# Splits of early projection rows, tap transposes and one rotary half moved in an attention and convolution layer pair

## The chip, the cores and the metric

The kernel runs on one core of a Trainium2 chip. The metric is the time of one execution on the device in microseconds (us). Before the change three runs took 1692.68 to 1693.34 us, with a median of 1692.94 us. Besides, one execution was taken by the hardware profiler; every row of a view below is from that one.

## The reference

Two layers work on 1024 latent tokens of width 1024, with a prefix of 256 context tokens. Layer 0 is an attention layer: 16 query heads of 128, four key and value heads (a group of four query heads shares one), a window of 128 tokens to each side, all context keys in the same softmax, a learned sink logit for each head, and rotary positions on latent queries and keys. Layer 1 is a convolution module of width 2048 with 31 taps. Each layer is normalised and modulated before its input projection, and a SiLU gate path multiplies its result before the output projection.

```python
def attention_layer(h_lat, h_ctx, w_in, sink, w_out, cos, sin, ctx_out):
    ...
    proj = h_lat @ w_in
    q = apply_rope(split_heads(proj[..., :q_end], N_Q_HEADS), cos, sin)
    k = apply_rope(split_heads(proj[..., q_end:k_end], N_KV_HEADS), cos, sin)
    ...
    o = windowed_attention(q, k, v, kc, vc, sink)
    y = (o * jax.nn.silu(z)) @ w_out
    return y, y_ctx
```

All inputs are float32. The kernel computes a product of two float32 matrices as three TensorE products: each operand is split into a high part, which is a rounded copy, and a low part, which is what the copy left out; then high times high, high times low and low times high are added up in one PSUM bank.

## The kernel before

**Engines and order.** TensorE (PE in the profile) multiplies and transposes, ScalarE (ACT) makes the rounded high copies and the exponentials, VectorE (DVE) the low parts, maxima and evacuations, GpSimd (POOL) the low parts of weights, the normalising of the softmax and most of the rotary arithmetic, SyncE (SP) issues nearly all DMAs. The order of PE's instructions is the order in which the program writes them (`pin`, L106). The orders on the other engines, after the start, are set by the planner of the framework, which runs a model of the engines' times at build time. The program can tie two instructions of one engine: `after` (L624) makes an instruction come behind a named one in that engine's queue. Each engine works its queue in order, so an instruction that waits holds all that stand behind it.

**Buffers.** Tiles of 128 x 1024 floats come from 45 pages, `pg` (L115), tiles of half that size from six half pages, `hp` (L116). Both hand out the page that has been free longest. PSUM has two banks `psg` for projections, two double banks `pss` for scores and transposed softmax rows, and two banks `pso`.

**The start.** Modulated inputs are made for the two halves of the latent tokens. For the second half a row of scales is spread over all partitions in the half page `rb` (L580); `x_f` (L455) reads it, and it is freed at L1184. The first head's query, key and value are projected here, and their rotary halves use the half pages too.

**The attention steps.** The loop at L1226 runs over 16 heads and eight blocks of 128 queries. A step writes on PE: the scores of the next block (`scores`, L1032), 12 matmuls of waiting work (`fill`, L1019), a value stage where one is due (`pv`, L1102), and the transposes of this block's softmax rows (`transposes`, L1068). After the transposes ACT copies the high part out of PSUM into `pthi`, and DVE writes the low part into `ptlo`; `anchor_a` and `anchor` name the last such pair of copies, `anchor_z` the two instructions that evacuate the latest half of a gate (L948). The waiting work is the projection of the next heads' queries and gates; `job` (L986) does 24 matmuls for each half of the tokens and calls `finish` (L934). For queries and keys that is `rope` (L896): ACT copies the bank, two DMAs swap the halves of a head, DVE multiplies by the cosine, POOL by the sine, then comes an addition and a low part. For queries after the first head both of the last two are on POOL. Where a new group of four heads begins (heads 4, 8 and 12) its key and value are projected in one go, 72 matmuls each.

**The output projection of layer 0** (`proj_attn`, L718) runs over four sub-sweeps `s` (half of the tokens by half of the columns) and eight row pairs `kk` of the weight; `i` counts both. `split(i)` (L735) makes the high part of a weight pair (`woh`) and, in the sub-sweeps where new rows of the attention's result come in, the high and low part of those rows (`ozh`, `ozl`), which were stored to DRAM and loaded again as `ozf`. `block` multiplies. The first seven row pairs (`EARLY_ROWS`) of the first sub-sweep begin early, as waiting work in the last head's steps: of their four blocks two are multiplied there (`early_proj`, L874), in the two banks `psg`, the other two afterwards. In that first pass `split(i + 1)` is written with the products of pair `i`.

**The taps.** The 31 taps of the convolution are loaded as rows and must be transposed. `turn_taps(q)` (L1298), four times, transposes four tiles of 32 rows into a bank `pso`, and DVE copies it into `dww`; the fourth time two sums follow. The four calls wait in the list `later`. `bgA` (L1800) is called after each row pair and takes up to two of them, from row pair 2 of a sub-sweep on. With two `pso` banks the third call needs a bank that the first has used.

Of the kernel before, what the change touches and what calls it, by code (L numbers as in the profile page):

```python
# [94 lines left out]
def backbone_kernel(  # L95
# [452 lines left out]
    for kt in range(2, KT):  # L548
        nx = kt + 1
        if 2 < kt < KT - 1:  # L550
            ada_row(nx)
            tp = turn(xs0, nx, ps_g)
        if kt == 5:
            root1 = rstd_root(ss1, D, 4)
        if kt == KT - 1:
            x_mm(kt - 1, 0, acc0, (2,))
            turn_vecs()
        x_mm(kt, 0, acc0, (0,))
        if nx < KT:
            ada_cols(nx)  # L560
            if kt == 5:
                r1 = rstd_end(root1, 4)
            x_tile(tp, nx, 0, V)
        else:
            x_h(0)
            x_f(1)
            x_l(0)
            rc = rstd_end(rootc, 2)
        x_mm(kt, 0, acc0, (1,) if nx < KT else (2, 1))
        if nx < KT:  # L570
            x_mm(kt - 1, 0, acc0, (2,), range(3) if kt > 2 else (1, 2))
        for i in {3: (0, 1), 4: (2, 3)}.get(kt, ()):
            square(xs1[i], ss1[:, i:i + 1], A)
        if kt == 4:
            pg.free(*xs1)
        if kt == 5:
            rps = ps_o(1)
            for b in range(4):
                PE.matmul(rps[:, b * P:b * P + P], r1[:, b:b + 1].to_broadcast([P, P]), ident, start=True, stop=True)
            rb_pg = hp.alloc(F32, None, "rb")  # L580
            rb1 = rb_pg[:, 0:512]
            act(rb1, rps, AF.Copy)
            for i in range(2):
                square(cx[i], ssc[:, i:i + 1], A)
        if kt == 6:
            pg.free(*xs0)
            cos, sin = (pg.alloc(F32, [1024], n) for n in ("cos", "sin"))
            SY.dma_start(out=cos, in_=k_cos)
            SY.dma_start(out=sin, in_=k_sin)
            rootc = rstd_root(ssc, D, 2)  # L590
            x_f(0)
# [126 lines left out]
    def proj_attn():  # L718

        st, oz = {}, {}  # L720
        todo = {"load": 0, "split": 0}

        def load(i):
            s, kk = seqB[i]
            h, m = subs[s]
            w, wl = pg.alloc(F32, [2, 512], "wo"), pg.alloc(F32R, [2, 512], "wol")
            SY.dma_start(out=w, in_=pair_rows(Wo, m, kk))
            SY.dma_start(out=wl.bitcast(F32), in_=wolA[m, kk])
            st[i] = [w, wl]
            if m == 0:  # L730
                f = pg.alloc(F32, [2, 512], "ozf")
                SY.dma_start(out=f, in_=ozd[2 * kk:2 * kk + 2, :, h * 512:h * 512 + 512].rearrange("a p n -> p a n"))
                oz[(h, kk)] = f

        def split(i):  # L735
            s, kk = seqB[i]
            h, m = subs[s]
            w, wl = st[i]
            wh = pg.alloc(F32R, [2, 512], "woh")
            act(wh, w, AF.Copy)  # L740
            pg.free(w)
            st[i] = (wh, wl)
            if m == 0:
                f = oz[(h, kk)]
                oh, ol = pg.alloc(F32R, [2, 512], "ozh"), pg.alloc(F32R, [2, 512], "ozl")
                after(act(oh, f, AF.Copy), anchor_z[0:1] if i else [])
                after(split_lo(V, ol, f, oh), anchor_z[1:2] if i else [])
                pg.free(f)
                oz[(h, kk)] = (oh, ol)

        def ahead(i, nl, ns):
            while todo["load"] <= min(i + nl, len(seqB) - 1):
                load(todo["load"])
                todo["load"] += 1
            while todo["split"] <= min(i + ns, len(seqB) - 1):
                split(todo["split"])
                todo["split"] += 1

        def block(s, kk, b, acc, w, o):
            for e in range(2):  # L760
                lh, ll = (t[:, e, b * P:b * P + P] for t in o)
                for a, c in ((lh, w[0]), (lh, w[1]), (ll, w[0])):
                    PE.matmul(acc, a, c[:, e], start=kk == 0 and e == 0 and a is lh and c is w[0],
                              stop=kk == NK - 1 and e == 1 and a is ll)
                    yield

        for i in range(EA):
            ahead(i, 0, -1)
            yield
        ahead(0, 1, 0)  # L770
        yield
        banks = {4: ps_g(), 5: ps_g()}
        for i in range(EARLY_ROWS):
            ahead(i, min(EA, EARLY_ROWS - 1 - i), min(1, EARLY_ROWS - 1 - i))
            for b in range(2):
                yield from block(0, i, b, banks[4 + b], st[i], oz[(0, i)])
        yield "early"
        ta, tb = ps_s(), ps_s()
        for i in range(4):
            banks[i] = (ta, tb)[i // 2][:, i % 2 * 512:i % 2 * 512 + 512]  # L780
        held = []
        xr = None
        for i, (s, kk) in enumerate(seqB):
            h, m = subs[s]
            acc = [banks[b] for b in ((4, 5, 0, 1), (2, 3, 4, 5), (0, 1, 4, 5), (2, 0, 3, 1))[s]]
            ahead(i, EA, 0)
            if kk == 4:
                xr = [pg.alloc(F32, [2, 512], "xr") for _ in range(2)]
                for b in range(4):
                    SY.dma_start(out=xr[b // 2][:, b % 2],  # L790
                                 in_=x[0, (4 * h + b) * P:(4 * h + b + 1) * P, m * 512:m * 512 + 512])
            w, o = st.pop(i), oz[(h, kk)]
            if i >= len(seqB) - BYBLOCK:
                ahead(i, EA, 1)
                held.append((kk, w, o))
                bgA(s, kk)
                if kk == NK - 1:
                    for b in range(4):
                        for k2, w, o in held:
                            run(block(s, k2, b, acc[b], w, o))  # L800
                        evac0(s, b, acc[b], xr)
                    for k2, w, o in held:
                        pg.free(*w, *o)
                continue
            for b in range(2 if i < EARLY_ROWS else 0, 4):
                run(block(s, kk, b, acc[b], w, o))
                if b == 2:
                    ahead(i, EA, 1)
            pg.free(*w)
            if m:  # L810
                pg.free(*oz.pop((h, kk)))
            bgA(s, kk)
            if kk == NK - 1:
                for b in range(4):
                    evac0(s, b, acc[b], xr)
# [77 lines left out]
            PE.matmul(o, wl[:, kt], Hh[kt][:, sl], start=False, stop=kt == KT - 1)  # L893
            yield

    def rope(o, sl, d, ropes=None, hold=None):  # L896
        qe, qs = (hp.alloc(F32, None, "rope") for _ in range(2))
        m = (hp if ropes is None else pg).alloc(F32, None, "rope")
        e, w, r = qe[:, 0:512], qs[:, 0:512], m[:, 0:512]
        act(e, o, AF.Copy)  # L900
        queue = A if ropes is None else SY
        queue.dma_start(out=w[0:64], in_=e[64:128])
        queue.dma_start(out=w[64:128], in_=e[0:64])
        first = tt(V, r, o, cos[:, sl], ALU.mult)
        tt(G, w, w, sin[:, sl], ALU.mult)

        def add(behind=None):
            i = tt(G if ropes is None and hold is None else V, r, r, w, ALU.add)
            if behind:
                after(i, [behind])  # L910
            act(d[0][:, sl], r, AF.Copy)

        def low():
            split_lo(G if ropes is None else V, d[1][:, sl], r, d[0][:, sl])
            hp.free(qe, qs)
            (hp if ropes is None else pg).free(m)

        def rest(behind):
            add(behind)
            low()  # L920

        if hold is not None:
            while hold:
                hold.pop()(first)
            hold.append(rest)
        elif ropes is None:
            add()
            low()
        else:
            ropes.extend((add, low))  # L930
# [3 lines left out]
    def finish(kind, n, half, o, d, ropes=None, hold=None):  # L934
# [8 lines left out]
                    hold.pop()(i)  # L943
                return None
        if kind in "qk":
            return rope(o, sl, d, ropes, hold)
        if kind == "z":
            anchor_z[:] = [act(d[:, sl], o, AF.Tanh, scale=0.5), stt(d[:, sl], d[:, sl], 1.0, o, ALU.add, ALU.mult)]  # L948
            return None
# [226 lines left out]
    for kt in range(KT):  # L1176
# [4 lines left out]
        if kt + 3 < KT:  # L1181
            x_f(kt + 3)
        if kt + 3 == KT - 1:
            hp.free(rb_pg)  # L1184
        if kt < 2:
            finished0(0, acc0, (kt,), ropes0)
        if kt > 3 and ropes0:
# [612 lines left out]
    def bgA(s, kk):  # L1800
        if s == 2 and kk == 6:
            wsB.load()
            wsB.load()
        if s == 3 and kk >= 5:
            wsB.split()
        for _ in range(2 if kk >= 2 else 0):
            if later:
                later.popleft()()

# [96 lines left out]
```

## Time and profile before

| | |
|---|---|
| median of three runs | 1692.94 us |
| the profiled execution, its own time | 1694.15 us |
| its span, from the first to the last instruction | 1692.4 us |
| TensorE busy | 1676.4 us (99%) |
| VectorE, ScalarE, GpSimd busy | 1115.4, 880.9 and 881.3 us |
| granted TensorE clock, mean | 0.998 |

A row of the timeline has the start in us from the beginning of the span, the duration in us, the engine, the line, the operation, the tiles (result, then operands), the shape, and how many like instructions the row stands for. In brackets stands how long the engine was idle before, and what released it. All instructions show L89, because a helper records them; they are told apart by their tiles. The list of waits gives the total in us, the number and the longest. The times of matmuls are pipelined and their ends are modelled, so one matmul overlaps the next.

### The profile page before, as it was taken

How to read it: one execution, taken by the hardware profiler on the slowest of the kernel's cores; microseconds unless marked ns; L12 is line 12 of the kernel's file. 1: busy time of each engine (PE TensorE's matmuls, PEld its weight loads, DVE VectorE, ACT ScalarE, POOL GpSimd, SP SyncE). 2: the span in 40 equal slices, each digit the busy share in tenths (PEclk: the TensorE clock that was granted, in tenths of full speed). 3: DMA queues.
4: the chain of work that ended last, by engine and by line, in shares of the span. 5: the costliest groups of instructions: out<-in, count | busy, mean ns of one | idle time of the engine just before them, and what ended most of it. 6: DMA issues, size and time to landing. Idle time of an engine off the chain costs nothing.

```text
span 1692.4 us, 23973 instructions
## 1 busy us (share of the span) xinstructions
PE 1676.4 (99%) x8436; PEld 1414.4 (84%) x8436; DVE 1115.4 (66%) x2120; ACT 880.9 (52%) x1556; POOL 881.3 (52%) x730
## 2 busy tenths in 40 slices
PE   9999999999999999999999999999999999999998
PEld 6788888888888888888788888888888888888886
DVE  4755554556356644566224289999999999868832
ACT  5755553555355543556234365555665654566741
POOL 0256663666466673652001268999898888130400
PEclk9999999999999999999999999999999999999999
DMA  9424442544344443447876623010211202377881
GB/s 387 148 80 143 143 126 84 163 144 141 92 139 151 147 133 99 134 136 247 288 253 220 229 82 101 13 64 25 75 50 51 82 32 82 126 272 245 315 292 50
DMA packets 114775, 244.54 MB, mean 144 GB/s; under 512 B 11626, under 2 KB 36514, under 8 KB 114656
## 3 DMA queue, kind: packets, MB, share of 16 engines
q1 hardware_dynamic: 108576, 233.06, 40.7%
q10 hardware_dynamic: 6080, 9.97, 2.4%
q8 instruction: 66, 1.08, 0.3%
q14 instruction: 53, 0.43, 0.1%
HBM read 190.80 MB, written 41.69 MB: 137 GB/s over the span
## 4 chain that ended last, share of the span: by engine, by line
PE 92%; DMA 4%; DVE 2%; ACT 1%; issue 0%; SPq 0%; POOL 0%; ACTq 0%; DVEq 0%; POOLq 0%
PE psg L89 49%; PE pss L89 23%; PE pso L89 21%; DMA x_page<-in_x_dram 1%; DMA x_page<-in_ctx_dram 1%; DMA araw_page<-in_k_ada_dram 1%; DMA wo_page<-in_attn_w_out_dram 0%; DMA rope_half<-rope_half 0%; DMA ozf_page<-ozd 0%; DVE hf_page L89 0%; DMA dww_raw<-in_ada_w_dram 0%; DVE ozl_page L89 0%; DVE oz_half L89 0%; ACT x_page L89 0%; ACT hh_page L89 0%
## 5 line engine op out<-in xcount | busy, mean ns | idle before, releaser
L89 POOL TENSOR_TENSOR odd_half<-odd_half,prod_half 128x513 f32<-128x513 f32 (+2 forms) x252 | 315.0, 1257 | 22.0 <-ACT prod_half L89 8.6
L89 PE MATMUL psg<-hh_page,whi_page 128*128 128x512 f32 x600 | 235.7, 393 | 0.0
L89 PE MATMUL psg<-hl_page,whi_page 128*128 128x512 f32 x600 | 234.7, 391 | 0.0
L89 PE MATMUL psg<-hh_page,wlo_page 128*128 128x512 f32 x600 | 234.2, 390 | 0.0
L89 POOL TENSOR_TENSOR wlo_page<-wraw_page,whi_page 128x512 fp32r<-128x512 f32 (+1 forms) x104 | 171.9, 1668 | 115.7 <-ACT whi_page L89 50.3
L89 ACT ACTIVATE prod_half<-ubuf,dww 128x513 f32<-128x513 f32 (+2 forms) x252 | 165.7, 675 | 115.8 <-POOL odd_half L89 111.9
L89 PE MATMUL psg<-h2h_page,whi_page 128*128 128x512 f32 x464 | 182.1, 392 | 0.0
L89 PE MATMUL psg<-h2h_page,wlo_page 128*128 128x512 f32 x464 | 180.9, 390 | 0.0
L89 PE MATMUL psg<-h2l_page,whi_page 128*128 128x512 f32 x464 | 180.8, 390 | 0.0
L89 POOL TENSOR_SCALAR p_page<-p_page,sc 128x640 f32<-128x640 f32 (+1 forms) x128 | 100.5, 786 | 148.6 <-DVE sc L89 134.2
L89 DVE SCALAR_TENSOR_TENSOR pss<-ubuf,dww,pss 128x512 f32<-128x512 f32 (+3 forms) x270 | 172.5, 671 | 0.1
L89 DVE SCALAR_TENSOR_TENSOR pss<-ubuf,wsum,pss 128x512 f32<-128x512 f32 (+3 forms) x270 | 171.8, 671 | 0.2
L89 ACT ACTIVATE p_page<-p_page,sc 128x641 f32<-128x641 f32 (+1 forms) x128 | 102.9, 804 | 93.2 <-DVE sc L89 90.3
L89 ACT ACTIVATE pthi<-pss 128x512 fp32r<-128x512 f32 (+2 forms) x144 | 87.4, 618 | 111.6 <-PE pss L89 108.0
L89 DVE TENSOR_TENSOR ptlo<-pss,pthi 128x512 fp32r<-128x512 f32 (+2 forms) x144 | 101.9, 716 | 63.0 <-ACT pthi L89 61.7
L89 PEld LDWEIGHTS psg<-hh_page,wlo_page 128*128 128x128 f32 x600 | 112.8, 188 | 24.4
L89 PEld LDWEIGHTS psg<-hh_page,whi_page 128*128 128x128 f32 x600 | 112.9, 188 | 19.2
L89 PEld LDWEIGHTS psg<-hl_page,whi_page 128*128 128x128 f32 x600 | 112.9, 188 | 18.4
L89 POOL TENSOR_TENSOR rope_half<-rope_half,sin_page 128x512 f32<-128x512 f32 x40 | 52.0, 1300 | 132.3 <-DMA rope_half<-rope_half 60.3
L89 ACT ACTIVATE whi_page<-wraw_page 128x1024 fp32r<-128x1024 f32 x88 | 92.6, 1052 | 51.1 <-PE psg L89 21.4
L89 PE MATMUL pso<-h2h_page,wlo_page 128*128 128x512 f32 x304 | 118.4, 389 | 0.0
L89 PE MATMUL pso<-h2h_page,whi_page 128*128 128x512 f32 x304 | 118.4, 389 | 0.0
(257 smaller groups left out, 4074.1 us busy)
## 6 DMA issues: line engine op xcount, KB each, us to landing
wraw_page<-in_k_wconv_dram SPq DMA_DIRECT2D x48, 512.0 KB, 3.3
wraw_page<-in_k_win_dram SPq DMA_DIRECT2D x40, 512.0 KB, 3.7
wo_page<-in_attn_w_out_dram SPq DMA_DIRECT2D x32, 512.0 KB, 5.7
wol_page<-wolA SPq DMA_DIRECT2D x32, 512.0 KB, 8.6
wo_page<-in_conv_w_out_dram SPq DMA_DIRECT2D x32, 512.0 KB, 7.2
wol_page<-wolC SPq DMA_DIRECT2D x32, 512.0 KB, 6.4
rope_half<-rope_half ACTq DMA_DIRECT2D x76, 128.0 KB, 2.3
araw_page<-in_k_ada_dram SPq DMA_DIRECT2D x16, 512.0 KB, 10.1
```

The source lines that it names most:

```text
L89: r = f(*a, **k)
```

## The change

- The row `rb` takes a full page instead of a half page.
- `split(i)` no longer ties the parts of the attention rows to the last gate half in every call but the first. For row pairs 1 to 6, and only these, the high part on ACT is tied behind the evacuation of the latest gate half and behind the latest `pthi` copy, the low part on DVE behind the second instruction of that evacuation and the latest `ptlo`.
- `rope` gets an engine for its addition and its low part. It is VectorE for the second half of the tokens of queries 4, 8 and 12, and GpSimd as before for the other queries.
- `bgA` takes from `later` in the first sub-sweep from row pair 0 on, so that the four tap transposes go with row pairs 0 and 1 instead of 2 and 3.

```diff
@@ -577,7 +577,7 @@
-            rb_pg = hp.alloc(F32, None, "rb")
+            rb_pg = pg.alloc(F32, [1024], "rb")
...
@@ -743,8 +743,11 @@
                 oh, ol = pg.alloc(F32R, [2, 512], "ozh"), pg.alloc(F32R, [2, 512], "ozl")
-                after(act(oh, f, AF.Copy), anchor_z[0:1] if i else [])
-                after(split_lo(V, ol, f, oh), anchor_z[1:2] if i else [])
+                high, low = act(oh, f, AF.Copy), split_lo(V, ol, f, oh)
+                if 0 < i < EARLY_ROWS:
+                    for ins, ties in ((high, (anchor_z[0:1], anchor_a)), (low, (anchor_z[1:2], anchor))):
+                        for t in ties:
+                            after(ins, t)
...
@@ -893,7 +896,7 @@
-    def rope(o, sl, d, ropes=None, hold=None):
+    def rope(o, sl, d, ropes=None, hold=None, eng=G):
...
@@ -905,13 +908,13 @@
-            i = tt(G if ropes is None and hold is None else V, r, r, w, ALU.add)
+            i = tt(eng if ropes is None and hold is None else V, r, r, w, ALU.add)
...
-            split_lo(G if ropes is None else V, d[1][:, sl], r, d[0][:, sl])
+            split_lo(eng if ropes is None else V, d[1][:, sl], r, d[0][:, sl])
...
@@ -943,7 +946,7 @@
-            return rope(o, sl, d, ropes, hold)
+            return rope(o, sl, d, ropes, hold, V if kind == "q" and half and n and n % 4 == 0 else G)
...
@@ -1181,7 +1184,7 @@
-            hp.free(rb_pg)
+            pg.free(rb_pg)
...
@@ -1803,7 +1806,7 @@
-        for _ in range(2 if kk >= 2 else 0):
+        for _ in range(2 if kk >= 2 or s == 0 else 0):
             if later:
                 later.popleft()()
```

## The prediction

> **What bounds the kernel now.** I read the page first, then the busy times by stretch, then who TensorE (PE) waited for, then the timeline around each wait.
>
> ```profile
> span 1692.4 us, 23973 instructions
> PE 1676.4 (99%) x8436; PEld 1414.4 (84%) x8436; DVE 1115.4 (66%) x2120; ACT 880.9 (52%) x1556; POOL 881.3 (52%) x730
> ```
>
> ```profile
> 0.00:45.00 45.00, 41.89 (x297) 29.40 (x297) 22.55 (x56) 26.99 (x42) 1.12 (x7) 1.00 0.97 388
> 772.00:831.00 59.00, 56.11 (x299) 46.79 (x298) 27.13 (x54) 26.96 (x41) 8.39 (x18) 1.00 0.81 269
> 831.00:1448.00 617.00, 617.00 (x2754) 511.15 (x2752) 505.01 (x822) 326.42 (x471) 422.65 (x310) 1.00 0.30 103
> 1530.00:1693.00 163.00, 154.37 (x706) 128.66 (x704) 89.87 (x173) 79.38 (x135) 23.48 (x16) 0.98 0.65 229
> ```
>
> The columns are the stretch, its length, and the busy time of PE, its weight loads, VectorE (DVE), ScalarE (ACT) and GpSimd (POOL), then the granted clock. PE is busy for 1676.4 of 1692.4 us, so only its 16 us of idle time, and what overlaps a modelled end, can be won. Of those, 8.63 us lie in the last stretch (163.00 - 154.37) and 3.11 in the first 45 us, where the change does almost nothing. From 831 to 1448 PE has no idle time at all. The one other stretch that loses is 772 to 831: 59.00 - 56.11 = 2.89 us. There the first row pairs of the output projection are mixed into the last attention steps. The pace of products of 512 columns, from the chain that ended last, is 43.52 / 192 = 0.227 us:
>
> ```profile
> 934.93 43.52 PE pss L89 x192
> ```
>
> ```profile
> PE pso L89 <- DVE dww L89: 1.4, 1, 1.4
> PE pss L89 <- DVE ptlo L89: 1.1, 1, 1.1
> PE pso L89 <- ACT hf_page L89: 0.8, 2, 0.6
> PE psg L89 <- DVE zs_page L89: 0.4, 1, 0.4
> ```
>
> Three of these waits, dww, ptlo and zs, are in that stretch. A wait is less exact than the distance between starts, so I price them by starts.
>
> **Row pairs 1 to 6: the splits behind the softmax copies.** PE, then ScalarE (ACT), then DVE:
>
> ```profile
> 230.84 0.59 PE L89 MATMUL pso<-mask_page,ones 128*1 128x256 f32 x2
> 231.36 0.39 PE L89 MATMUL pss<-kh_page,qh_page 128*128 128x256 f32 x1
> ...
> 780.85 0.71 PE L89 MATMUL pss<-ident,p_page 128*128 128x128 f32 x5
> ...
> 786.32 0.59 PE L89 MATMUL pso<-mask_page,ones 128*1 128x256 f32 x2
> 788.00 0.44 PE L89 MATMUL pss<-kh_page,qh_page 128*128 128x384 f32 x1 [1.09 <-DVE ptlo L89]
> ...
> 791.71 0.40 PE L89 MATMUL pso<-pthi,kvc_page 128*128 128x512 f32 x1
> 792.18 0.51 PE L89 MATMUL pso<-ptlo,kvc_page 128*128 128x512 f32 x1
> ```
>
> ```profile
> 783.31 1.99 ACT L89 ACTIVATE ozh_page<-ozf_page 128x1024 fp32r<-128x1024 f32 x2
> 785.21 0.68 ACT L89 ACTIVATE pthi<-pss 128x640 fp32r<-128x640 f32 x1
> ```
>
> ```profile
> 784.85 2.36 DVE L89 TENSOR_TENSOR ozl_page<-ozf_page,ozh_page 128x1024 fp32r<-128x1024 f32 x2
> 787.12 0.82 DVE L89 TENSOR_TENSOR ptlo<-pss,pthi 128x640 fp32r<-128x640 f32 x1
> ...
> 791.32 0.81 DVE L89 TENSOR_TENSOR ptlo<-pss,pthi 128x640 fp32r<-128x640 f32 x1
> ```
>
> PE's scores at 788.00 wait for `ptlo`, the low softmax copy of a step that PE had transposed by 781.6. It is late because ACT ran two row-pair splits (`ozh`, 1.99 us) ahead of the high copy `pthi`, and DVE two more (`ozl`, 2.36 us) ahead of `ptlo`. The new ties keep each split of pairs 1 to 6 behind both copies of the step emitted last. So `pthi` can run where ACT started `ozh`, from 783.3 to 784.0, and `ptlo` where DVE started `ozl`, from 784.85 to 785.7: before the scores want the bank at 786.9. Price: the two small products and the scores start 0.52 us apart at 230.84 and 1.68 us apart at 786.32, so **1.16 us** goes. The next step's `ptlo` (791.32 to 792.13) also holds the second product of the value stage: 0.47 us between starts where undisturbed ones are 0.23 apart; **0.24 us** goes.
>
> The zs wait stays, I think. Its cause is ACT's queue before the evacuation of the last gate half, and no tied instruction stands there; it could go (0.4 us by the wait row) or grow by a `pthi` (0.68 us) slipping ahead of it. I take 0.
>
> What the added wait costs: behind a split waiting for `pthi` on ACT stand the exponentials and the weight splits; behind `ozl` on DVE the maxima. PE wants each split about one step later. The tightest is pair 5, tied behind this `ptlo` and first read by the third product of its block:
>
> ```profile
> 804.87 0.82 DVE L89 TENSOR_TENSOR ptlo<-pss,pthi 128x640 fp32r<-128x640 f32 x1 [1.33 <-ACT pthi L89]
> ```
>
> ```profile
> 807.60 0.40 PE L89 MATMUL psg<-woh_page,ozl_page 128*128 128x512 f32 x1
> ```
>
> 804.87 + 0.82 + 1.23 (one `ozl`, row 828.31 below) = 806.9, against 807.6: 0.7 us to spare. If a weight split of 1.06 us (of the form of row 827.22 below) goes between, PE loses about 0.4 us. The bounds are 0 and one such slip for each of pairs 3, 4 and 5, 1.2 us; I take 0.1, since the trace already runs pairs 5 and 6 in that order without a wait. Dropping the ties of pair 7 and of the second half costs nothing: the gate half they named is that of the zs wait, over long before.
>
> **Taps with row pairs 0 and 1.**
>
> ```profile
> 824.49 0.39 PE L89 MATMUL pss<-woh_page,ozl_page 128*128 128x512 f32 x1
> 824.80 0.68 PE L89 MATMUL pso<-ident,dwr_page 32*128 32x32 f32 x8
> ...
> 828.04 0.39 PE L89 MATMUL pss<-woh_page,ozl_page 128*128 128x512 f32 x1
> 829.78 0.68 PE L89 MATMUL pso<-ident,dwr_page 32*128 32x32 f32 x8 [1.36 <-DVE dww L89]
> ```
>
> ```profile
> 827.22 1.06 ACT L89 ACTIVATE ozh_page<-ozf_page 128x1024 fp32r<-128x1024 f32 x1 [2.64 <-DMA ozf_page<-ozd]
> ```
>
> ```profile
> 828.31 1.23 DVE L89 TENSOR_TENSOR ozl_page<-ozf_page,ozh_page 128x1024 fp32r<-128x1024 f32 x1 [10.12 <-ACT ozh_page L89]
> 829.45 0.47 DVE L89 COPY dww<-pso 128x124 f32<-128x124 f32 x2
> ```
>
> ```profile
> 821.15 0.36 SPq L89 DMA_DIRECT2D ozf_page<-ozd  x1
> ```
>
> The transposes themselves are kept: 16 matmul records on PE, four copies and two sums on DVE, no DMA. The first two groups start 0.31 us after the product in front of them, the last two 1.74 us: **1.43 us** is waiting for a bank that the first groups' copies free. The copies are late because DVE's queue holds the `ozl` of pair 7 first; its data were read back from DRAM only from 821.15 on, landed at 827.2, and DVE sat idle for 10.12 us. In the new place each group passes the second halves of two row pairs (24 products) on PE. The 36 products before 824.80 began at about 816.6, so the first two groups end near 816.6 + 12 x 0.227 + 0.6 = 819.9; their copies need 0.47 us of that idle DVE time, and when PE comes to the last two, at 822.6, the bank is free. The last two copies may still stand behind pair 7, but by the code PE asks for their banks next in the third quarter of the projection. SP's and POOL's queues are not passed; the two pages of raw taps are freed two pairs earlier. What is late next is pair 7's `ozl`, ending at 829.54 and wanted 36 products after 830.4, at 838.6: with PE 2.7 us earlier, 6 us remain.
>
> **Second half of queries 4, 8 and 12 on VectorE.** Add and low split leave GpSimd (POOL), three times.
>
> ```profile
> 241.33 1.29 POOL L89 TENSOR_TENSOR rope_half<-rope_half,rope_half 128x512 f32<-128x512 f32 x1
> ...
> 251.04 2.99 POOL L89 TENSOR_TENSOR wlo_page<-wraw_page,whi_page 128x512 fp32r<-128x512 f32 x2
> ```
>
> ```profile
> 240.60 0.69 DVE L89 TENSOR_TENSOR rope_half<-psg,cos_page 128x512 f32<-128x512 f32 x1 [3.17 <-ACT rope_half L89]
> 247.10 0.69 DVE L89 TENSOR_TENSOR rope_half<-rope_half,rope_half 128x512 f32<-128x512 f32 x1 [0.49 <-POOL rope_half L89]
> 251.12 1.76 DVE L89 TENSOR_TENSOR rope_half<-rope_half,rope_half 128x512 f32<-128x512 f32 x1 [0.24 <-POOL rope_half L89]
> ```
>
> ```profile
> 234.26 13.79 PE psg L89 x72
> ```
>
> POOL gives up 6 x 1.29 = 7.7 us. DVE takes 6 x 0.69 = 4.1 us when alone. Beside POOL the same add took 1.76 us (251.12, while POOL's two instructions took 2.99), so at most 10.6 us. DVE has the room: it idles 3.17 us before 240.60. What is exposed is the cosine product behind it in DVE's queue, which frees the bank that the context part of the keys wants at 234.26 + 48 x 0.227 = 245.1. The add can start when POOL's sine product ends (241.3) and the low split after ACT's copy, which in the worst order (0.69 + about 0.7 + 0.69) moves the product from 240.6 to 243.4; it ends at 244.1, hidden by 1 us. If that cover went, PE would lose up to 1 us in each of three places. The keys and queries themselves are wanted after the values' 72 products as well, at 234.26 + 2 x 13.79 = 261.8 or later. I take 0; the bounds are 0, because no PE wait stands there that it could remove, and +3.0.
>
> [...]
>
> **The row `rb` in a full page.** No instruction is added. Of six half pages five instead of six are held at the peak, and the 45 full pages have at least six free there by the code's order of allocations. The only waits near are `hf` (0.8 us in two), so the bounds are -0.8 and +0.8; I take 0, because what those await is arithmetic on ACT and DVE, not a page.
>
> **The sum.** -1.16 - 0.24 + 0.1 - 1.43 = -2.7 us, kept to the end since PE has no idle time from 831 to 1448 and DVE's work there begins with PE's. The profiled execution took 1694.15 us (span 1692.4); it would take 1691.4. The median of the runs shown is 1692.94, so the forecast is **1690.2 us**.
>
> **Rivals.**
> *The taps' copies stay behind pair 7 on DVE.* Then moving the taps makes PE stand at the third group from 822.6 until 829.54 + 0.3: 7.2 us instead of 1.43, so +5.8 - 1.3 = +4.5 us, 1697.4. It decides by one thing: whether DVE's queue has that `ozl` ahead of the first copies, as it has now. Against it, the taps come ready 5.5 us earlier while pair 7 still has a write and a read of DRAM in front of it. [...] The clock is 1.00 through every wait here; no run shown has such a stall.
>
> *Another filler takes the place of the splits.*
>
> ```profile
> 790.67 2.23 ACT L89 ACTIVATE woh_page<-wo_page 128x1024 fp32r<-128x1024 f32 x2 [1.18 <-DVE ozl_page L89]
> ```
>
> The weight splits are not tied. If one of these goes ahead of the next `pthi`, that copy ends about 792.4 and its `ptlo` 793.2, where PE wants it at 790.6: 2.4 us, so the ties win nothing: 1692.9 - 1.4 + 1.0 = about 1692.5. A milder form, late splits of pairs 3 to 5, gives 1691.4.
>
> *More goes.* The zs wait (0.4) goes too, and one of the two `hf` waits with the moved page (0.4): -3.5, 1689.4.
>
> **How the numbers follow.** About 0.2%, 3.4 us, is what a measurement of this kernel can tell from no change. Forecast 0.55 (own range 1689.6 to 1690.9, all within 0.2%); fillers or late splits 0.14 (within); more goes 0.14 (faster); taps behind pair 7, or reordered queues that stall as long, 0.17 (slower). So faster 0.14, same 0.69, slower 0.17. The range 1689.2 to 1692.8 leaves out the slow case and the far end of the fast one, under 0.2.
>
> **What would show it.** Right: the PE waits lose dww and ptlo; `pthi` and `ptlo` stand ahead of each `ozh` and `ozl` of pairs 1 to 6; dww copies begin near 818.5, ahead of pair 7's `ozl`; 772 to 831 holds under 0.7 us of PE idle; nothing new near 245, 434 and 623. Wrong: a PE wait for dww of several us, a PE wait for `ozl` or `pthi` between 785 and 812, or a new PE wait after 831.

## The result, and the profile after

| | before | after |
|---|---|---|
| median of 21 runs each, taken side by side | 1693.23 us | 1691.12 us |
| lowest to highest | 1691.91 to 1695.93 us | 1690.08 to 1692.68 us |
| span of the profiled execution | 1692.4 us | 1689.8 us |

The ratio of the runs is 0.9985, with a 95% interval of 0.9978 to 0.9991: the change saves 1.5 to 3.7 us, 2.1 by the medians. The interval leaves out no change, but by the medians it is less than the 0.2% that I had set as the bound. 2.7 us were forecast. As a time, 1691.12 us lies 0.2 us above the range that I had given the forecast itself, 1689.6 to 1690.9, and inside the wide one.

The busy times by stretch of the changed kernel, in the columns of before's:

```profile
0.00:45.00 45.00, 41.61 (x293) 29.22 (x294) 22.52 (x56) 26.75 (x42) 1.12 (x7) 1.00 0.97 387
772.00:831.00 59.00, 59.00 (x315) 49.94 (x314) 28.31 (x54) 27.54 (x41) 8.02 (x18) 1.00 0.84 286
831.00:1448.00 617.00, 617.00 (x2753) 510.86 (x2753) 507.54 (x825) 328.62 (x475) 422.64 (x310) 1.00 0.30 102
1530.00:1690.00 160.00, 151.36 (x692) 125.91 (x690) 90.32 (x171) 78.27 (x133) 24.25 (x16) 0.99 0.65 231
```

From 772 to 831 PE is busy for all 59.00 us, where it had 56.11 before: 2.89 us, a little more than the whole difference of the spans (2.6). From 831 to 1448 it has no idle time, as before, so what was won was carried that far. At the two ends some of it is given back: in the first 45 us PE idles 3.39 us instead of 3.11, and from 1530 to the end of the span 8.4 instead of 8.0 us (the last window runs past the end of the span, here by 0.2 us and before by 0.6). Who PE waited for in the changed kernel:

```profile
PE pso L89 <- ACT hf_page L89: 0.9, 2, 0.6
PE pso L89 <- DVE r L89: 0.6, 1, 0.6
PE pso L89 <- DVE oz_half L89: 0.5, 3, 0.2
```

The waits for dww, ptlo and zs are gone, the two for hf stand, and one for r is new (more on it below). The places of before, in the timeline of PE, of ScalarE and of VectorE:

```profile
786.12 0.59 PE L89 MATMUL pso<-mask_page,ones 128*1 128x256 f32 x2
786.64 0.44 PE L89 MATMUL pss<-kh_page,qh_page 128*128 128x384 f32 x1
...
790.37 0.40 PE L89 MATMUL pso<-pthi,kvc_page 128*128 128x512 f32 x1
790.60 0.39 PE L89 MATMUL pso<-ptlo,kvc_page 128*128 128x512 f32 x1
```

```profile
782.97 0.69 ACT L89 ACTIVATE pthi<-pss 128x640 fp32r<-128x640 f32 x1
783.55 1.05 ACT L89 ACTIVATE ozh_page<-ozf_page 128x1024 fp32r<-128x1024 f32 x1
```

```profile
784.51 0.82 DVE L89 TENSOR_TENSOR ptlo<-pss,pthi 128x640 fp32r<-128x640 f32 x1
785.24 1.22 DVE L89 TENSOR_TENSOR ozl_page<-ozf_page,ozh_page 128x1024 fp32r<-128x1024 f32 x1
...
804.13 1.23 DVE L89 TENSOR_TENSOR ozl_page<-ozf_page,ozh_page 128x1024 fp32r<-128x1024 f32 x1
...
818.15 0.54 DVE L89 COPY dww<-pso 128x124 f32<-128x124 f32 x2 [1.65 <-PE pso L89]
821.70 0.54 DVE L89 COPY dww<-pso 128x124 f32<-128x124 f32 x2 [3.02 <-PE pso L89]
...
827.10 1.23 DVE L89 TENSOR_TENSOR ozl_page<-ozf_page,ozh_page 128x1024 fp32r<-128x1024 f32 x1 [4.34 <-ACT ozh_page L89]
```

The scores follow the small products by 0.52 us (1.68 before), the second product of the value stage follows the first by 0.23 us. `pthi` runs at 782.97 ahead of `ozh`, where two `ozh` had stood; `ptlo` starts at 784.51 instead of 787.12. All four copies into `dww` are done at 822.2, ahead of pair 7's `ozl` at 827.10. Pair 5's `ozl`, the tightest of the late splits, ends at 805.36, 0.55 us ahead of the product at 805.91 that reads it first.

### The profile page after: what moved, and what is told of

It reads as the page before. It is cut to its first block, busy times and chain, and to the rows that moved or that the text cites. A ratio compares the mean times of both kernels' runs of the same rounds, so it can differ in the third digit from the quotient of the medians.

```text
span 1689.8 us, 23975 instructions
## 1 busy us (share of the span) xinstructions
PE 1676.0 (99%) x8436; PEld 1413.9 (84%) x8436; DVE 1120.5 (66%) x2126; ACT 881.6 (52%) x1556; POOL 874.3 (52%) x724
## 4 chain that ended last, share of the span: by engine, by line
PE 92%; DMA 4%; DVE 2%; ACT 1%; issue 1%; SPq 0%; DVEq 0%; ACTq 0%
PE psg L89 50%; PE pss L89 21%; PE pso L89 21%; DMA wo_page<-in_conv_w_out_dram 1%; DMA araw_page<-in_k_ada_dram 1%; DMA x_page<-in_ctx_dram 1%; DMA x_page<-in_x_dram 1%; DVE pso L89 1%; DVE v_page L89 1%; DMA zsd<-sig_page 0%; DVE hf_page L89 0%; DMA wsum_raw<-in_ada_w_dram 0%; SPq L89 0%; ACT hh_page L89 0%; ACT gs_page L89 0%
## 5 line engine op out<-in xcount | busy, mean ns | idle before, releaser
L89 PE MATMUL pso<-h2l_page,whi_page 128*128 128x512 f32 x304 | 118.3, 389 | 0.0
```

Of the source, the lines that this page charges most:

```text
L89: r = f(*a, **k)
```

## The experiments

My theory was that PE's waits are the whole of it, and that each of the two larger edits takes away its own. The rivals: the two quiet edits (rotary halves, the page for `rb`) carry part of the gain, or the profile of before had caught an unusual execution. In this first round each kernel was profiled once, so its waits are those of one execution; medians and ratios are against runs of before on the same chip.

### The ties alone, the taps alone, both, and the two quiet edits alone

Four kernels, each made of before and of the parts of the change that its name tells. The lines that decide:

```diff
+                if 0 < i < EARLY_ROWS:
...
+        for _ in range(2 if kk >= 2 or s == 0 else 0):
...
+            rb_pg = pg.alloc(F32, [1024], "rb")
...
+            return rope(o, sl, d, ropes, hold, V if kind == "q" and half and n and n % 4 == 0 else G)
```

The first stands for the ties, the second for the taps, the last two for the quiet edits.

> The kernel before with the ties of row pairs 1 to 6 alone. Theory (PE's waits are the whole of it, each edit takes away its own): the PE waits for ptlo (1.1 us) and zs (0.4) go, the wait for dww (1.4) stays; between 772 and 831 PE is busy about 57.6 of 59 us, and the span is 1.2 to 1.9 us shorter than before's. Rival (the quiet edits bring part of it: the zs wait went with the moved rotary half, since ScalarE's queue was rearranged by it): the zs wait of 0.4 is still there, and the span is at most 1.4 us shorter.

> The kernel before with the taps moved to row pairs 0 and 1 alone. Theory: the PE wait for dww (1.4 us) goes, the waits for ptlo (1.1) and zs (0.4) stay; the first copies into dww stand ahead of pair 7's ozl on VectorE without any tie; the span is 1.4 us shorter than before's. Rival (the copies come first only because the ties freed VectorE earlier): a wait for dww stays, up to 7 us long, and the span is longer by up to 5.8 us.

> The changed kernel without the rotary halves on VectorE and without the full page for rb. Theory: the same as the changed kernel within what can be told, the waits for dww, ptlo and zs all gone, 2.6 us less span than before, and the new PE wait for r near 1561 (0.6) is there as well, since it comes from PE arriving earlier. Rival (a quiet edit carries part): the span stands 0.4 us or more off that of the changed kernel, by a wait that can be named, or the wait for r is not there.

> The kernel before with the two quiet edits alone: second halves of queries 4, 8 and 12 on VectorE, and rb in a full page. Theory: all waits of before stay (dww 1.4, ptlo 1.1, zs 0.4, hf 0.8), nothing new near 245, 434 and 623, and the span is that of before within 0.3 us. Rival (they bring or cost something): a PE wait for psg or the keys of up to 1 us in each of three places, or the zs or hf wait gone, so between 0.8 us shorter and 3.0 us longer.

| kernel | median | ratio to before, 95% | span | PE waits for dww / ptlo / zs |
|---|---|---|---|---|
| ties alone | 1691.87 us | 0.9991 [0.9982, 1.0000] | 1690.5 us | 1.1 / 0 / 0 us |
| taps alone | 1692.59 us | 0.9995 [0.9986, 1.0004] | 1691.0 us | 0 / 1.1 / 0.3 us |
| both | 1691.56 us | 0.9989 [0.9980, 0.9997] | 1690.3 us | 0 / 0 / 0 us |
| quiet edits alone | 1692.58 us | 0.9996 [0.9987, 1.0005] | 1690.4 us | **0** / 1.1 / **0** us |

The ties take away the ptlo wait and the taps the dww wait, each as expected. In the kernel with the taps alone the copies come first without a tie, so they do not need the ties. Both together give the time of the whole change (1691.56 us against 1691.12), so the quiet edits bring nothing that can be told. One thing there is not as expected: the wait for r near 1561 is absent, and one of 1.1 us for x near 972 is there, which puts the span 0.5 us above the changed kernel's; the changed kernel has the same in its second profile below. But the fourth line breaks the theory. Without ties and with the taps in their old place, the waits for dww and zs are gone too, and the span is 2.0 us shorter than before's. PE's and SP's orders there are those of before, and the orders of VectorE and ScalarE around the taps as well. What differs is when pair 7's rows landed. ScalarE, VectorE and PE with the quiet edits alone:

```profile
825.21 1.06 ACT L89 ACTIVATE ozh_page<-ozf_page 128x1024 fp32r<-128x1024 f32 x1 [0.91 <-DMA ozf_page<-ozd]
```

```profile
826.30 1.23 DVE L89 TENSOR_TENSOR ozl_page<-ozf_page,ozh_page 128x1024 fp32r<-128x1024 f32 x1 [8.53 <-ACT ozh_page L89]
827.45 0.47 DVE L89 COPY dww<-pso 128x124 f32<-128x124 f32 x2
```

```profile
827.95 0.68 PE L89 MATMUL pso<-ident,dwr_page 32*128 32x32 f32 x8
```

The load was issued at 820.42 and ScalarE could start at 825.21, 4.8 us later; in before's profile it took 6.1 us (821.15 to 827.22). The `ozl` still stands ahead of the copies, but it ends at 827.5, and PE's third group at 827.95 waits for nothing. Either the dww wait is a draw of each execution, or the quiet edits moved it.

### Before, after and the quiet edits, profiled again

> The kernel before, unchanged, profiled once more. Theory (the wait for dww and the zs wait hang on when a load lands, and are a draw of each execution; only the ptlo wait belongs to the order of the queues): the ptlo wait stands at 1.1 us again, while the dww wait is anywhere between 0 and 1.5 us by the time pair 7's ozf lands (started by ScalarE 6.1 us after its issue in the first profile of before, 4.8 with the quiet edits), and the zs wait between 0 and 0.5 us by the landing of the weight pair ahead of it; the span is 1690.4 to 1692.4 us. Rival (both waits belong to before's queues and the quiet edits took them away): dww 1.4 us and zs 0.4 us again, and the span within 0.3 us of 1692.4.

> The changed kernel, unchanged, profiled once more. Theory: no PE wait for dww, ptlo or zs in this execution either, between 772 and 831 PE is busy for all 59 us, and what was given back near 1561 (a wait for r of 0.6 us) is a draw that may be away; the span is 1689 to 1690.5 us. Rival (the first profile was a lucky one): one of the three waits is there, or PE idles 0.5 us or more between 772 and 831.

> The kernel with the two quiet edits alone, profiled once more. In its first profile the wait for dww was away, with the same order of queues around the taps as before's two profiles, which had 1.4 and 1.5 us. Theory (the wait hangs on how long the read of pair 7's rows takes: ScalarE could start on them 4.8 us after the issue there, 6.1 and 6.4 us in before's two): whichever way it comes out, the dww wait follows that time, near 0 at 4.8 us or less, and 1 us or more at 6 us; ptlo waits as in before. Rival (the quiet edits take the dww wait away): no dww wait, even if that time is 5.7 us or more.

> The kernel before, unchanged, profiled a third time, beside the run above. Theory: the ptlo wait of 1.0 to 1.1 us is there; the dww wait follows the time from the issue of pair 7's read to ScalarE's start on it (0 to 1.5 us); a spell of products 0.43 us apart behind the dww wait, as in the second profile, may or may not come. Rival (the dww wait is fixed in before's order): 1.4 to 1.5 us whatever that time is.

| kernel (taps in the old place) | from the issue of the load to ScalarE's start | PE waits for dww |
|---|---|---|
| before, first profile | 6.07 us | 1.36 us |
| before, second | 6.39 us | 1.45 us |
| before, third | 4.98 us | 0 |
| ties alone | 6.00 us | 1.10 us |
| quiet edits alone, first | 4.79 us | 0 |
| quiet edits alone, second | 6.09 us | 0.99 us |

The same kernel has the wait in one execution and not in another, and it follows the time of the load. To be exact, it follows the time from PE's first group of taps to ScalarE's start on pair 7's rows: 2.42, 2.50, 2.16 and 2.04 us in the four executions with a wait (in the table's order), 1.02 and 0.81 in the two without, and each wait is that time less 1.05 or 1.06 us. So a PE that comes late hides part of it: in the third profile of before the first group started 0.4 us later than in the other two. Of six executions four have the wait, and the mean is 0.8 us. That settles it: **the dww wait is a draw, and the moved taps take the draw away**. With the taps at row pairs 0 and 1 the load took 4.2 to 6.1 us in six profiles, and PE waited in none.

The third profile of before lost nothing at the taps, but 0.9 us more than the first one in the value stage; the second lost at both places. PE in the second and third profiles of before:

```profile
786.88 0.44 PE L89 MATMUL pss<-kh_page,qh_page 128*128 128x384 f32 x1 [0.97 <-DVE ptlo L89]
792.17 0.50 PE L89 MATMUL pso<-ptlo,kvc_page 128*128 128x512 f32 x1 [1.18 <-DVE ptlo L89]
```

```profile
787.52 0.44 PE L89 MATMUL pss<-kh_page,qh_page 128*128 128x384 f32 x1 [1.06 <-DVE ptlo L89]
792.57 0.50 PE L89 MATMUL pso<-ptlo,kvc_page 128*128 128x512 f32 x1 [0.94 <-DVE ptlo L89]
```

The wait ahead of the scores is the steady one: 0.97 to 1.09 us in the six profiles without ties. The wait in the value stage, 0.24 us in the first profile, is 1.18 and 0.94 us here: an `ozh` of the next pair had to wait 1.12 and 0.63 us for its load on ScalarE, ahead of the `pthi` of that step. The ties take that draw away as well: in all seven profiles with ties the two products start 0.23 or 0.24 us apart.

The medians were 1693.17 and 1694.44 us for before (ratios 0.9999 [0.9988, 1.0009] and 1.0001 [0.9991, 1.0011]), 1693.19 for the quiet edits (0.9993 [0.9983, 1.0003]) and 1691.28 for the change (0.9989 [0.9979, 0.9999]). The second profile of before has a span of 1694.0 us, above the 1690.4 to 1692.4 that I expected: it has both draws and a spell of slow clock (last section). The second profile of the change has a span of 1690.2 us and no idle PE from 772 to 831. It has no wait for r either, but one for x of 1.1 us. VectorE, GpSimd and PE in it:

```profile
963.57 2.93 DVE L89 TENSOR_TENSOR x_page<-x_page,xr_page 128x512 f32<-128x512 f32 x1
```

```profile
963.56 5.21 POOL L89 TENSOR_TENSOR wlo_page<-wraw_page,whi_page 128x1024 fp32r<-128x1024 f32 x2 [29.02 <-DMA wraw_page<-in_k_wconv_dram]
```

```profile
972.10 0.50 PE L89 MATMUL pss<-woh_page,ozh_page 128*128 128x512 f32 x1 [1.14 <-DVE x_page L89]
```

VectorE's addition of two SBUF tiles began 0.01 us after GpSimd's first instruction of the pair and took 2.93 us. In the first profile of the change it began at 963.85, 0.21 us ahead of GpSimd, and took 0.69 us; PE then waited for nothing. The long time came where GpSimd began first: in the second profile of the change and in that of both edits it did, by 0.01 and 0.02 us, and the addition ended 2.94 and 2.95 us after GpSimd's start; in seven other profiles (the first ones of before, of the change and of the quiet edits, the ties alone, the taps alone, and the two further steps below) the addition began first, by 0.04 to 0.22 us, and took 0.68 or 0.69 us. The wait, 1.0 to 1.1 us, came in the second profile of the change, with both edits alone, in the third of before and in the second of the quiet edits: it is no part of the change.

### The slower rival, made true

```diff
+        ahead(0, EARLY_ROWS, EARLY_ROWS)
         for i, (s, kk) in enumerate(seqB):
...
-        V.tensor_copy(dww[:, q * 4:q * 4 + 4, :], ...)
+        c = V.tensor_copy(dww[:, q * 4:q * 4 + 4, :], ...)
+        if q == 0:
+            after(c, low7)
```

The new call loads and splits pair 7 ahead of the main rows; `low7` holds its low part's instruction.

> The slower rival of the prediction made true: the changed kernel, with pair 7 loaded and split ahead of the main rows in the program and the first copy into dww tied behind pair 7's ozl on VectorE. PE must then stand at the third group of tap transposes from about 822 until that ozl ends, 828.3 in the changed kernel's profile, 6 to 7 us. Theory: one PE wait for dww of 5.5 to 7 us, nothing won back later, so 5 to 7 us slower than the changed kernel, near 1697 us. Second reading: part of it is won back because later stages are paced by other engines, so under 4 us slower. [...]

1706.65 us, 1.0077 [1.0061, 1.0092] of before, span 1705.5: 15.4 us more than the change on the same chip, about twice what I had said. SP, ScalarE, VectorE and PE:

```profile
827.23 0.37 SPq L89 DMA_DIRECT2D ozf_page<-ozd  x1
```

```profile
831.98 1.06 ACT L89 ACTIVATE ozh_page<-ozf_page 128x1024 fp32r<-128x1024 f32 x1 [8.74 <-DMA ozf_page<-ozd]
```

```profile
833.07 1.23 DVE L89 TENSOR_TENSOR ozl_page<-ozf_page,ozh_page 128x1024 fp32r<-128x1024 f32 x1 [13.32 <-ACT ozh_page L89]
834.21 0.28 DVE L89 COPY dww<-pso 128x124 f32<-128x124 f32 x1
```

```profile
834.59 1.03 PE L89 MATMUL pso<-ident,dwr_page 32*128 32x32 f32 x8 [12.22 <-issue]
...
838.28 0.63 PE L89 MATMUL pss<-woh_page,ozh_page 128*128 128x512 f32 x1
838.71 0.63 PE L89 MATMUL pss<-wol_page,ozh_page 128*128 128x512 f32 x1
```

PE stands for 12.2 us. The view names no releaser (`issue`), but the rows do: the tied copy stands behind pair 7's `ozl` and ends at 834.5, and PE's third group starts at 834.59. The mechanism is the rival's, but its price hangs on the load, which I had held fixed at 821.3. With the split written earlier, SP's order changed with it: loads of `xr`, of which four had gone out at 805.4, now go out from 817.8 to 821.1, among the last three writes of `ozd`, which leave from 818.6 on instead of from 812.3 on. The read of pair 7 goes out at 827.23, 8.5 us after PE's first group of taps instead of 3.6. Without these 4.9 us PE would stand for 7.3 us, an estimate. Nearly all of the rest is the clock. The busy times by stretch of this kernel, granted clock third from the end:

```profile
834.00:836.00 2.00, 1.41 (x9) 1.38 (x10) 1.08 (x5) 0.00 (x0) 0.00 (x0) 0.50 0.00 1
838.00:840.00 2.00, 2.00 (x7) 1.52 (x6) 0.00 (x0) 0.00 (x0) 0.00 (x0) 0.50 0.15 59
840.00:842.00 2.00, 2.00 (x7) 1.58 (x6) 0.00 (x0) 0.92 (x1) 0.00 (x0) 0.59 0.14 15
842.00:844.00 2.00, 2.00 (x11) 1.63 (x10) 0.00 (x0) 0.19 (x2) 0.00 (x0) 1.00 0.82 275
```

Products start 0.43 us apart instead of 0.227 until 841.5, for 7 us after the wait: 14 of them, so 2.8 us. With the slow transposes in front it is 3.1 us: from the third group to the 15th product behind it PE takes 7.09 us, and 3.95 in the first profile of before. 12.2 and 3.1 are 15.3 of the 15.4 us. From 842 on the granted clock is 1.00 again. The 3.1 us were not in the 5 to 7 that I had given.

### Two further steps

The waits for `oz_half` (three of 0.2 us by the wait rows, 0.33 by starts) stand where a new group's values are turned through the bank that the value stage has just filled. In the first kernel they are turned one step later:

```diff
             scores(*nxt)
-            vlate.pop(g)()
+            turned.append(vlate.pop(g))
             continue
...
         if nxt and not regroup:
             scores(*nxt)
+        if turned:
+            turned.pop()()
```

The second one also takes three low parts off GpSimd, one of which had begun just ahead of VectorE's addition where that took 2.93 us:

```diff
-lo_eng=lambda i: V if i < 2 or i % 3 == 0 and i > 3 else G
+lo_eng=lambda i: V if i < 5 or i % 3 == 0 else G
```

> The changed kernel, with the second half of each new group's values turned one step later (behind the next scores instead of directly behind the value stage that has just filled the same bank). Theory: the three waits for oz_half near 267, 456 and 645, 0.33 us each by starts, go and nothing takes their place, so 1.0 us shorter than the changed kernel. Rival (the copies of the turned values then stand ahead of the softmax copies of that step): the three waits turn into waits for ptlo or p of 0.3 us or more, and the time is the same or longer.

> The kernel with the values turned one step later, and with the low parts of three weights of the convolution's input projection (the third to the fifth) on VectorE instead of GpSimd. In two profiles VectorE's addition at 963.6 began 0.01 to 0.02 us after one of these GpSimd instructions, took 2.93 instead of 0.69 us, and PE then waited 1.3 us for x at 972; where it began 0.04 us or more before GpSimd's it took 0.69 and PE waited for nothing. Theory: that addition takes 0.69 us and no wait for x_page near 972 can come, so on the mean of executions 0.3 to 0.6 us shorter than with the values later alone, near 1690.2 us. Rival (VectorE now has 3.7 us more to do in the place where it evacuates): a wait of PE for x_page or hf of 0.5 us or more between 965 and 1005, and no gain.

The first: 1690.62 us, 0.9985 [0.9977, 0.9994] of before, span 1688.4. The three waits are gone and nothing stands in their place there; the zs wait of 0.4 us is back in this execution, with the ties in force. Against the change on the same chip (1691.28) it is 0.7 us less by the medians, which these runs alone can't tell from nothing; the vanished rows can: by starts each of the places is 0.3 us shorter. The second: 1689.42 us, **0.9969 [0.9958, 0.9980]** of before (1694.59 us on that chip), span 1687.6, the lowest of all profiles here, and its runs lie within 1688.43 to 1689.77. By the medians that is 5.2 us below before, where the first step had 2.8: more than the 0.3 to 0.6 us that I expected of the second edit, but the two intervals still overlap. Who PE waited for there, all rows, VectorE's addition and GpSimd:

```profile
PE pss L89 <- DVE zerr_page L89: 2.0, 1, 2.0
PE pss L89 <- DVE hl_page L89: 1.3, 3, 0.6
PE pso L89 <- ACT hf_page L89: 0.9, 2, 0.6
PE pso L89 <- DMA araw_page<-in_k_ada_dram: 0.4, 1, 0.4
PE pss L89 <- ACT hh_page L89: 0.2, 1, 0.2
```

```profile
965.27 0.68 DVE L89 TENSOR_TENSOR x_page<-x_page,xr_page 128x512 f32<-128x512 f32 x1
```

```profile
965.49 2.73 POOL L89 TENSOR_TENSOR wlo_page<-wraw_page,whi_page 128x1024 fp32r<-128x1024 f32 x1 [31.97 <-DVE wlo_page L89]
```

No wait is left after the first 70 us, and the addition takes 0.68 us. One profile doesn't show that the draw at 972 can't come. GpSimd still begins a low part 0.22 us behind the addition, but the row says that VectorE's `wlo` released it, and that instruction stands directly ahead of the addition in VectorE's queue (964.14 to 965.36). So in this execution the two did not race. The runs spread over 1.3 us instead of before's 5.3, but they are seven against 23. The edit's own worth isn't shown either: the addition took 0.69 us in the profile of the first step too, and the 0.8 us between the two spans are the zs wait (0.4) and the first 45 us (3.93 and 3.49 us of idle PE), both ahead of the place of the edit.

## Why the prediction was right, and which terms were off

The forecast was -2.7 us; measured were -2.1 us by medians, -2.6 by the spans of the two profiles shown, with 1.5 to 3.7 as the interval. The bottleneck, the stretch, the order of the queues and the signs of the terms hold; the sizes of single terms hold less well than the sum. One of the things that were to show the forecast wrong did come, a new PE wait after 831 (below).

- **Where PE idles.** Misread in two places, without harm to the sum: the 8.63 us of the last stretch hold 0.6 us that lie behind the end of the span, and 772 to 831 was not the only other stretch that lost. From 45 to 772 PE idled 1.93 us, the waits for hf and oz_half among them; the first further step takes part of that.
- **Scores behind `ptlo`, -1.16.** Right: 0.97 to 1.09 us by the wait rows in every profile without ties, none with them.
- **Second product of the value stage, -0.24.** Mis-sized: 0.24 us between starts beyond the usual in four of the six profiles without ties, but 1.35 and 1.11 us in the other two (before's second and third). The mean is 0.57 us. I had taken one profile's figure for the kernel's.
- **Taps, -1.43.** Mis-sized the other way, by the same fault: 0 to 1.45 us by the draw, 0.8 on the mean. The row in brackets, which named the load of `ozf` as what ScalarE waited for, was the sign that this term could vary, and I gave it no range.
- **Late splits, +0.1.** None seen in the five profiles with both edits: from 772 to 831 PE is busy throughout, or idles only for zs. Pair 5 had 0.55 us to spare where 0.7 were worked out.
- **The zs wait, "stays, I take 0".** It went in the first profile of the change. But that is a draw too: it was there in the first profile of before, with the taps alone and in the changed kernel with the values later, and away in the second and third of before. The ties don't decide it; the landing of the weight pair ahead of it on ScalarE does. ScalarE idled 2.60 to 2.65 us for that load in the three profiles with the wait, and 1.7 to 2.3 us in all others.
- **Rotary halves and `rb`, 0 each.** Both together bring nothing that can be told: 0.9996 [0.9987, 1.0005] and 0.9993 [0.9983, 1.0003] alone, and no wait near 245, 434 and 623. They were not tried one by one. In the first place of the changed kernel the worst order came, the cosine product started at 243.94 (243.4 was worked out), and it was hidden as said. The six moved instructions took 0.69 us each, so 4.1 us and not 10.6.
- **"Kept to the end".** Right as a rule, with draws on the way: the wait for r at 1561 (0.6 us) in the first profile of the change, the wait for x near 972 (1.1 us) in the second. Neither was in the forecast; the one for x comes in before too, the one for r in the first profile of the change alone.
- **The slower rival.** It did not come: without any tie the planner put the copies first in each kernel with the taps at row pairs 0 and 1. Its price was never met on its own terms: in the run that made it true PE stood for 12.2 us instead of 7.2, because SP's order moved with the split, and 7.3 us would be left without that. The slow clock behind the wait, 3.1 us in that run, is not in the price of +4.5 us.

So the sum came out right partly because two errors of one kind, -0.24 for about -0.6 and -1.43 for about -0.8, cancel. That is luck.

What stays open: why the read of pair 7 takes 4.2 to 6.4 us, and what sets the wait for r; no run was made for either.

## What to carry to other kernels

A wait that ends on a load can be a draw (the one for dww was 0 to 1.45 us in six profiles): profile the kernel before two or three times, or give the term the whole range from zero to its size, before you add it to a sum. An instruction that waits for a load in an engine's queue holds all that stand behind it, so a late load shows as a wait for something else (in the first profile of before VectorE idled 10.12 us ahead of pair 7's `ozl`, the `dww` copies stood behind it, and PE waited 1.36 us for them); tying such instructions behind what the bottleneck engine needs next, and moving what stood behind the load, bought a steadier time (21 runs within 2.6 us instead of 4.0), even though the median moved by little. When a split is moved, look at the DMAs that it brings along: the tie cost 12 us instead of about 7 because a read went out 5 us later.

## What the runs showed of the hardware that was not expected

The granted clock fell once behind a short wait. PE's products behind the taps, and the stretches there, in the second profile of before:

```profile
829.86 0.68 PE L89 MATMUL pso<-ident,dwr_page 32*128 32x32 f32 x8 [1.45 <-DVE dww L89]
831.49 0.63 PE L89 MATMUL pss<-woh_page,ozl_page 128*128 128x512 f32 x1
831.92 0.63 PE L89 MATMUL pss<-woh_page,ozh_page 128*128 128x512 f32 x1
...
834.20 0.39 PE L89 MATMUL pss<-woh_page,ozh_page 128*128 128x512 f32 x1
834.43 0.40 PE L89 MATMUL pss<-wol_page,ozh_page 128*128 128x512 f32 x1
```

```profile
829.00:831.00 2.00, 1.14 (x9) 1.07 (x10) 1.63 (x7) 1.24 (x2) 0.00 (x0) 0.86 0.69 214
831.00:834.00 3.00, 3.00 (x9) 2.31 (x8) 0.39 (x2) 0.00 (x0) 0.00 (x0) 0.52 0.94 313
834.00:836.00 2.00, 2.00 (x10) 1.66 (x9) 0.00 (x0) 0.00 (x0) 0.00 (x0) 1.00 1.00 383
```

After a wait of 1.45 us, with small transposes on both sides of it, the granted clock is 0.52 for 3 us and seven products start 0.43 us apart: about 1.5 us more, as much again as the wait. The first profile of before has the same transposes and a wait of 1.36 us, and no such spell: its granted clock is 1.00 from 829 to 836. PE did not stand for long in either: in the second profile it was busy 2.41 of 3.00 us from 826 to 829 and 1.14 of 2.00 from 829 to 831, and the longest stretch without a product, transposes included, is 2.06 us, and 1.97 in the first profile. What set the spell off in one execution and not in the other isn't shown.

And a start 0.01 us later on one engine cost 2.2 us there and 1.1 us on PE (VectorE's addition at 963.57 in the second profile of the change). Of a time that moves by 0.1% from run to run, such draws are a part that a profile can name.
